# Twelve dense steps instead of eight between the levels of a GLA pair, levels in turn on VectorE, the first pair's output after the second pair's states, v copies at high priority

## The chip, the cores and the metric

The kernel runs on one core of a Trainium2 chip. The metric is the device time of one execution in microseconds; the time before is the median of three runs. Engines are called as in the profile: PE (TensorE), DVE (VectorE), ACT (ScalarE), POOL (GpSimd), SP (the queue that issues DMAs here).

## The reference

One layer of a bidirectional encoder, applied to two batches with the same weights: a prompt of 256 tokens and a sample of 512 tokens, width 1024.

```python
h = rmsnorm(x, norm1[l])
(gq, gk, gv, gg, glr, dq, dk, dvv, sz, sxbc, sdt) = jnp.split(h @ w_in[l], IN_OFFSETS, axis=-1)
...
x = x + jnp.concatenate([o_gla, o_diff, o_ssd], axis=-1) @ w_out[l]
h = rmsnorm(x, norm2[l])
x = x + jnp.square(jax.nn.relu(h @ w_mlp1[l])) @ w_mlp2[l]
```

Three mixers stand between `w_in` and `w_out`. The one that the change is about is `o_gla`: gated linear attention with four heads, forward and backward, in which each pair of tokens i, j is weighted by a decay for each of 64 channels:

```python
b = jnp.cumsum(gi, axis=1)
diff = b[:, :, None] - b[:, None, :]
decay = jnp.exp(jnp.where(mask[:, :, None, None], diff, -jnp.inf))
attn = jnp.einsum('bihd,bjhd,bijhd->bijh', qi, ki, decay)
```

`o_diff` is a differential attention with softmax, whose v comes from the columns `dvv`; `o_ssd` is a state space mixer behind a convolution over five tokens. Everything is float32.

## The kernel before

All 768 tokens of both batches lie side by side, as six tiles of 128 tokens (`NT`, `T`). A product with a weight is made of three matmuls in float32r on a high and a low part of both operands (`mm3`, L97 to L101).

**Dense steps.** `tm_steps` (L212) is a generator: for one unit of 256 weight columns it yields after each of the six token tiles, that is after 8 x 3 = 24 matmuls. Two tiles share one accumulator, of which there are three (`psa`, `N_ACC`, L52; `fm_unit`, which makes the convolution's products, takes from the same three), and after each second step a consumer takes the accumulator away. Four such units are chained in `rest` (L1125): the output gates of the two GLA pairs (consumer `gcons`: a tanh on ACT and a product on DVE, at high priority) and the v of the two differential pairs (`diff_v`, L825; consumer `vcons`: a copy on ACT into a tile, and a store of it to memory by SP). What `rest` has left is drawn by `diff_in` (L822) behind its own q and k units.

**GLA levels.** The heads are worked on in two pairs. `gla_within` (L408) makes the attention inside a chunk of 128 tokens in seven levels, s = 64, 32, 16, 8, 4, 2, 1, and once more for the diagonal. A level subtracts a reference from the two prefix sums (`d`, L452, two buffers of pool `d2`), takes exponentials on ACT (L463, L472), multiplies q and k by them on DVE (`eq` L464, `ek` L473, from pool `t3` with four buffers), and then multiplies small blocks on PE (`blocks`, L428: 96 matmuls of 32 columns for each of the two heads). `into_local` (L346) puts the result into `L` on DVE. Before the blocks of each level `other()` (L414) draws one dense step from `rest`; a list, `order`, ties step and blocks to each other in this order on PE. A pair draws eight steps, so two pairs draw sixteen of the 24: all twelve of the gates and four of the first v unit.

**Order.** Each engine works through its queue in the order that a planner gives it at build time. It takes the program's order as priority and its own model of durations; a block marked `tc.high_priority()` comes ahead of its place, `tc.issue_after(ins)` keeps the instructions traced inside behind `ins` on the engine of `ins`.

**Tiles that the change touches.** The pool `in` (`i3`, L69) has twelve tiles. While the second pair's levels run they hold v, q and k of the second pair (four) and the gates of both pairs (four); a copy of v in `vcons` takes one until its store has landed. Later each consumer of `diff_in` (L802) takes two, a raw and a squared one, and the convolution (L612, L623) takes two for each of its six tiles. The output of a pair is `gla_out` (L525): twelve products on DVE (L530), twelve transposes, four scalings on ACT, four stores. The states of a pair are `gla_states` (L348). In the program (L1126 to L1132) the first pair's output stands between the second pair's levels and the second pair's states.

After that come the differential attention of the prompt (`diff_in` and `diff_head` for two pairs of heads), the convolution, the state space mixer, the output product, the MLP of the prompt, and the same for the sample.

Of the kernel before, what the change touches and what calls it, by code (L numbers as in the profile page):

```python
# [14 lines left out]
AF = mybir.ActivationFunctionType  # L15
ALU = mybir.AluOpType
# [4 lines left out]
P = 128  # L21
D = 1024
KT = D // P
NT = 6
T = NT * P
# [18 lines left out]
def hybrid_kernel(ctx, tc, io):  # L44
    nc = tc.nc
    mm, act, dve, pool = nc.tensor.matmul, nc.scalar, nc.vector, nc.gpsimd
# [41 lines left out]
    def mx(name):  # L88
        return psm.tile([P, 512], F32, tag="mx", name=nm(name))
# [4 lines left out]
    def bc(ap, shape):  # L94
        return ap.to_broadcast(shape)
# [57 lines left out]
    def in_unit(c0, n=256):  # L153
        return load_unit(lambda r: [(0, n, w_in[:, r, c0:c0 + n])], (KT, n))
# [57 lines left out]
    def tm_steps(load, consume):  # L212


        w = load()
        for t0 in range(0, NT, 2):
            ps = acc("tm")
            for i in range(2):
                ts = slice((t0 + i) * P, (t0 + i + 1) * P)
                for k in range(KT):  # L220
                    last = mm3(ps[:, i * 256:(i + 1) * 256], tuple(z[:, ts] for z in hT[k]),
                               (w[0][:, k, :], w[1][:, k, :]), k == 0, k == KT - 1)
                if i == 1:
                    consume(ps.rearrange("p (t c) -> p t c", t=2), t0)
                yield last
# [35 lines left out]
    def v128(t):  # L261
        return t.rearrange("p (c w) -> p c w", w=P)
# [42 lines left out]
    def gla_v(hp):  # L305
        v = [i3("gv") for _ in range(2)]

        def vcons(ps, t0):
            with tc.high_priority():
                for h in range(2):  # L310
                    act.copy(v128(v[h])[:, t0:t0 + 2, :], ps[:, :, h * P:(h + 1) * P])

        tm_unit(in_unit(C_GV + 2 * hp * P), vcons)
        return v
# [29 lines left out]
    def into_local(L, ps, i):  # L344

        dve.copy_predicated(L, bc(masks[:, i, None, :], [P, NT, 32]), ps)  # L346
# [61 lines left out]
    def gla_within(pre, qk, rest):  # L408

        Xf, Xb, _ = pre  # L410
        q, k = qk
        order = []

        def other():  # L414
            with ExitStack() as behind:
                for ins in order[-1:]:
                    behind.enter_context(tc.issue_after(ins))
                order.append(next(rest))

        A = [v128(c4("A", n=T)) for _ in range(2)]
        L = t2("L", n=12 * 32).rearrange("p (h c i) -> p h c i", h=2, c=NT)
        pool.memset(L, 0.0)
        k3 = v128(k)

        def blocks(ps, h, w, left, right, across):  # L428

            hs = slice(64 * h, 64 * h + 64)  # L430
            with tc.issue_after(order[-1]):
                for c in range(NT):
                    for b in range(P // w):
                        o = b ^ across
                        last = mm(ps[w * b:w * b + w, c, :], lhsT=left[hs, c, w * b:w * b + w],
                                  rhs=right[hs, c, w * o:w * o + w], start=True, stop=True)
            order.append(last.ins)

        for li, s in enumerate(LEVELS):
            nb = T // (2 * s)  # L440
            d = d2("d")

            def parts(t):

                return t.rearrange("p (b r i) -> p b r i", r=2, i=s)

            D = [parts(d[:, i * T:(i + 1) * T]) for i in range(2)]

            for i, X in enumerate((Xb, Xf)):
                x = parts(X)  # L450
                ref = x[:, :, 1, 0:1] if i == 0 else x[:, :, 0, s - 1:s]
                dve.tensor_tensor(D[i].rearrange("p b r i -> p b (r i)"), X.rearrange("p (b i) -> p b i", i=2 * s),  # L452
                                  bc(ref, [P, nb, 2 * s]), ALU.subtract)
            eq = t3("eq")

            def halves(t):
                return t.rearrange("p (b r i) -> p r b i", r=2, i=s)

            if s <= 32:

                own = d[:, :2 * (T + s)].rearrange("p (r x) -> p r x", r=2)[:, :, :T]
                own = own.rearrange("p r (b i) -> p r b i", i=2 * s)[:, :, :, :s]
                act.activation(own, own, AF.Exp, scale=-0.0625)  # L463
                dve.tensor_tensor(halves(eq), own, halves(q), ALU.mult)  # L464
            else:
                for i in range(2):
                    act.activation(D[i][:, :, i], D[i][:, :, i], AF.Exp, scale=-0.0625)
                    dve.tensor_tensor(parts(eq)[:, :, i], D[i][:, :, i], parts(q)[:, :, i], ALU.mult)
            if s > 1:
                ek = t3("ek")  # L470
                for i in range(2):
                    act.activation(D[1 - i][:, :, i], D[1 - i][:, :, i], AF.Exp, scale=0.0625)  # L472
                    dve.tensor_tensor(parts(ek)[:, :, i], D[1 - i][:, :, i], parts(k)[:, :, i], ALU.mult)  # L473
            else:
                ek = k
            left, right = v128(ek), v128(eq)
            other()
            if s == 64:
                for h in range(2):
                    ps = mx("att")[:, :NT * 64].rearrange("p (c i) -> p c i", c=NT)  # L480
                    blocks(ps, h, 64, left, right, 1)
                    act.copy(A[h][0:64, :, 64:128], ps[0:64])
                    act.copy(A[h][64:128, :, 0:64], ps[64:128])
                continue
            for h in range(2):
                ps = mx("att")[:, :NT * 32].rearrange("p (c i) -> p c i", c=NT)
                blocks(ps, h, 32, left, right, int(s == 32))
                if s < 32:
                    into_local(L[:, h], ps, LOCAL.index(s))
                    continue  # L490
                for b in range(4):
                    o = 32 * (b ^ 1)
                    act.copy(A[h][32 * b:32 * b + 32, :, o:o + 32], ps[32 * b:32 * b + 32])

        q2 = t3("q2")
        act.activation(q2, q, AF.Copy, scale=2.0)
        other()
        for h in range(2):
            ps = mx("att")[:, :NT * 32].rearrange("p (c i) -> p c i", c=NT)
            blocks(ps, h, 32, k3, v128(q2), 0)  # L500
            into_local(L[:, h], ps, LOCAL.index(0))
            for b in range(4):
                act.copy(A[h][32 * b:32 * b + 32, :, 32 * b:32 * b + 32], L[32 * b:32 * b + 32, h])

        return A

# [18 lines left out]
    def gla_out(hp, core, sg):  # L525
        o_sb, rs = core
        for h in range(2):
            for c in range(NT):
                ov = v128(o_sb[h])[:, c, :]
                dve.scalar_tensor_tensor(ov, ov, rs[:, h, c:c + 1], v128(sg[h])[:, c, :], op0=ALU.mult, op1=ALU.mult)  # L530
            oT = t3("oT")
            for (a, b) in ((0, 4), (4, 6)):
                ps = mx("goT")
                for c in range(a, b):
                    nc.tensor.transpose(ps[:, (c - a) * P:(c - a + 1) * P], v128(o_sb[h])[:, c, :], ident)
                act.activation(oT[:, a * P:b * P], ps[:, :(b - a) * P], AF.Copy, scale=half[:, 40:41])
            for sq, (a, b) in enumerate(SEQS):
                nc.sync.dma_start(out=mixg[sq][2 * hp + h], in_=oT[:, a * P:b * P])
# [286 lines left out]
    def diff_v(p):  # L825
        def vcons(ps, t0):
            v = i3("dv", n=512).rearrange("p (t c) -> p t c", t=2)
            act.copy(v, ps)  # L828
            nc.sync.dma_start(out=dvd[p][t0 // 2], in_=v)
        return tm_steps(lambda: in_unit(C_DV + 256 * p), vcons)  # L830

# [184 lines left out]
    v = gla_v(0)  # L1016
# [67 lines left out]
    pre = [gla_gates(hp) for hp in range(2)]  # L1084
# [36 lines left out]
    states = gla_states(pre[0], qk, v)  # L1121
    qk1, v1 = gla_qk(1), gla_v(1)
    gates = [gla_gate_out(hp) for hp in range(2)]
    v_steps = [diff_v(p) for p in range(2)]
    rest = chain(gates[0][1], gates[1][1], *v_steps)  # L1125
    A = gla_within(pre[0], qk, rest)  # L1126
    core = gla_sum(A, states, v)
    A = gla_within(pre[1], qk1, rest)
    gla_out(0, core, gates[0][0])
    states = gla_states(pre[1], qk1, v1)  # L1130
    core = gla_sum(A, states, v1)
    gla_out(1, core, gates[1][0])  # L1132

# [122 lines left out]
    def feature_tiles(t):  # L1256

        return [tuple(z[:, 256 * (k % 4):256 * (k % 4) + 256] for z in B[f"{k // 4 + 1}{t + 1}"]) for k in range(KT)]

    halves = [feature_tiles(t) for t in range(2)]  # L1260
# [169 lines left out]
```

## Time and profile before

| | |
|---|---|
| time before | 1137.02 us, median of three (1133.65 to 1139.05) |
| profiled execution | 1138.52 us, its span 1136.7 us |
| granted clock of PE, mean | 0.983 |
| PE busy | 1086.8 us, 96% of the span |
| PE weight loads busy | 986.5 us, 87% |
| DVE busy | 804.3 us, 71% |
| ACT busy | 622.3 us, 55% |
| POOL busy | 126.8 us, 11% |

The page gives one execution. Busy time of PE is modelled, since matmuls overlap; what tells more is where PE is idle, what ended the idle time, and which clock was granted (1.0 is 2.4 GHz, 0.5 is 1.2 GHz). A row in which two numbers stand ahead of the engine begins with the start and the duration in us; a count follows x; an idle time ahead of an instruction stands in brackets with the instruction that ended it.

### The profile page before, as it was taken

The page shows a single profiled execution, that of the slowest core. Times are in us where ns is not written, and L with a number is a line of the kernel's source. Part 1 is how long each engine was busy: PE and PEld are TensorE (multiplying, and loading weights), DVE is VectorE, ACT ScalarE, POOL GpSimd, SP SyncE. Part 2 cuts the span into 40 slices and gives each one's busy share as a digit, 9 for nine tenths or more (in the row PEclk, how much of TensorE's full clock was granted, in tenths as well). Part 3 has the DMA queues.
Part 4 walks back from the last instruction along what each step waited for, and adds up shares of the span by engine and source line. Part 5 has one row for each costly group of instructions (what it writes and reads, how often), then busy time and mean ns, then how long its engine had stood idle before and what let it go on. Part 6 is the DMA issues. An engine that isn't in the chain of part 4 may idle for free.

```text
span 1136.7 us, 20939 instructions
## 1 busy us (share of the span) xinstructions
PE 1086.8 (96%) x8372; PEld 986.5 (87%) x8372; DVE 804.3 (71%) x1414; ACT 622.3 (55%) x1216; POOL 126.8 (11%) x184
## 2 busy tenths in 40 slices
PE   7999879999999998899999999998999999999998
PEld 7999779999889986788878897787988998998997
DVE  6579975474687577887687787756886756756752
ACT  7487574664267236756766673434544543543541
POOL 1001012220400280110101102200000000000000
PEclk9999898999999999899999999999999999999999
DMA  6212101172425355345545457642252342242212
GB/s 201 87 42 76 40 22 67 38 232 73 130 83 152 104 172 171 112 148 170 184 139 176 159 175 257 214 148 74 96 185 76 93 126 78 93 131 74 93 38 74
DMA packets 118647, 136.49 MB, mean 120 GB/s; under 512 B 8935, under 2 KB 86789, under 8 KB 118549
## 3 DMA queue, kind: packets, MB, share of 16 engines
q1 hardware_dynamic: 118517, 135.14, 37.6%
q8 instruction: 66, 1.08, 0.4%
q14 instruction: 32, 0.26, 0.1%
q10 hardware_dynamic: 32, 0.01, 0.0%
HBM read 121.44 MB, written 13.68 MB: 119 GB/s over the span
## 4 chain that ended last, share of the span: by engine, by line
PE 66%; DVE 13%; DMA 10%; ACT 7%; issue 2%; POOL 1%; SPq 0%; ACTq 0%; DVEq 0%; POOLq 0%
PE tp L99 8%; PE tp L100 8%; PE tp L101 8%; PE X L1288 7%; DMA wr<-in_w_mlp 5%; PE tm L99 4%; PE tm L101 4%; PE tm L100 4%; PE fm L99 4%; PE fm L100 3%; PE Z L1288 3%; PE fm L101 3%; DVE wl L136 3%; ACT wh L135 2%; DMA er<-scr 2%
## 5 line engine op out<-in xcount | busy, mean ns | idle before, releaser
L136 DVE TENSOR_TENSOR wl<-wr,wh 128x1024 fp32r<-128x1024 f32 x130 | 160.0, 1245 | 65.1 <-ACT wh L135 64.7
L135 ACT CAST wh<-wr 128x1024 fp32r<-128x1024 f32 x138 | 141.7, 1049 | 108.4 <-DMA wr<-in_w_mlp 58.8
L99 PE MATMUL tm<-wh,hTh 128*128 128x256 f32 x576 | 166.5, 290 | 0.9 <-ACT xp L620 0.8
L101 PE MATMUL tm<-wh,hTl 128*128 128x256 f32 x576 | 166.0, 289 | 0.0
L100 PE MATMUL tm<-wl,hTh 128*128 128x256 f32 x576 | 164.5, 286 | 0.0
L99 PEld LDWEIGHTS tm<-wh,hTh 128*128 128x128 f32 x576 | 110.6, 192 | 3.0 <-ACT xp L620 1.0
L100 PEld LDWEIGHTS tm<-wl,hTh 128*128 128x128 f32 x576 | 110.9, 193 | 0.4 <-DVE wl L136 0.2
L101 PEld LDWEIGHTS tm<-wh,hTl 128*128 128x128 f32 x576 | 110.6, 192 | 0.1
L1381 DVE TENSOR_TENSOR xres<-tp,xres 128x512 f32<-128x512 f32 x56 | 38.6, 690 | 55.1 <-PE tp L101 54.6
L99 PE MATMUL fm<-h,wh 128*128 128x256 f32 x256 | 71.7, 282 | 1.8 <-ACT relu L993 1.8
L100 PE MATMUL fm<-h,wh 128*128 128x256 f32 x256 | 71.8, 282 | 0.0
L101 PE MATMUL fm<-h,wl 128*128 128x256 f32 x256 | 71.1, 282 | 0.6 <-DVE wl L136 0.6
L99 PE MATMUL fm<-hTh,wh 128*128 128x384 f32 x160 | 55.8, 349 | 2.8 <-ACT dv L828 2.6
L100 PE MATMUL fm<-hTl,wh 128*128 128x384 f32 x160 | 55.0, 343 | 0.0
L101 PE MATMUL fm<-hTh,wl 128*128 128x384 f32 x160 | 54.7, 342 | 0.0
L947 DVE TENSOR_TENSOR xres<-tp,xres 128x512 f32<-128x512 f32 x60 | 40.3, 685 | 16.3 <-PE tp L101 16.2
L100 PE MATMUL tp<-wl,u 128*128 128x512 f32 x128 | 51.0, 398 | 0.5 <-DVE wl L136 0.5
L99 PE MATMUL tp<-wh,u 128*128 128x512 f32 x128 | 49.8, 401 | 0.9 <-ACT wh L135 0.8
L101 PE MATMUL tp<-wh,u 128*128 128x512 f32 x128 | 50.6, 395 | 0.0
L99 PEld LDWEIGHTS fm<-h,wh 128*128 128x128 f32 x256 | 48.2, 188 | 2.5 <-ACT relu L993 2.1
L101 PEld LDWEIGHTS fm<-h,wl 128*128 128x128 f32 x256 | 47.8, 188 | 1.0 <-DVE wl L136 0.8
L100 PEld LDWEIGHTS fm<-h,wh 128*128 128x128 f32 x256 | 48.2, 188 | 0.6
(429 smaller groups left out, 3089.3 us busy)
## 6 DMA issues: line engine op xcount, KB each, us to landing
wr<-in_w_mlp SPq DMA_DIRECT2D x100, 512.0 KB
wr<-in_w_in SPq DMA_DIRECT2D x30, 512.0 KB
wb<-in_w_mlp SPq DMA_DIRECT2D x28, 512.0 KB
wr<-in_w_out SPq DMA_DIRECT2D x24, 512.0 KB
ar<-scr SPq DMA_DIRECT2D x6, 512.0 KB
er<-scr SPq DMA_DIRECT2D x6, 512.0 KB
x<-in_x_sample SPq DMA_DIRECT2D x4, 512.0 KB
wr<-in_w_in SPq DMA_DIRECT2D x8, 256.0 KB
```

The lines of the kernel that those rows point to most:

```text
L99: mm(out, lhsT=lh, rhs=rh, start=first, stop=False)
L100: mm(out, lhsT=lh, rhs=rl, start=False, stop=False)
L101: return mm(out, lhsT=ll, rhs=rh, start=False, stop=last).ins
L135: act.copy(hi, raw)
L136: dve.tensor_tensor(lo, raw, rd(hi), ALU.subtract)
L947: dve.tensor_tensor(xres[t][:, cs], ps, xres[t][:, cs], ALU.add)
L1288: mm(out, lhsT=a[l][:, k, c], rhs=b[r][:, k, :], start=first and j == k == z == 0, stop=j == 1 and k == 3 and z == 2, skip_group_check=True)
L1381: dve.tensor_tensor(xres[t][:, cs], ps, xres[t][:, cs], ALU.add)
```

## The change

`other()` is called twice before the blocks of the levels s = 16, 8, 4 and 2, so a pair draws twelve steps and the two pairs draw all 24; `diff_in` finds `rest` empty. A list `ends` keeps the last DVE multiply of each level: the subtractions of a level are issued behind the last multiply of the level before last, the multiplies of q behind the last multiply of the level before. The copy of v from its accumulator gets high priority. `gla_out` of the first pair stands after `gla_states` of the second.

```diff
-        order = []
+        order, ends = [], []
+
+        def behind(n):
+
+            return tc.issue_after(ends[-n]) if len(ends) >= n else ExitStack()
...
-                dve.tensor_tensor(D[i].rearrange("p b r i -> p b (r i)"), X.rearrange("p (b i) -> p b i", i=2 * s),
-                                  bc(ref, [P, nb, 2 * s]), ALU.subtract)
+                with behind(2):
+                    dve.tensor_tensor(D[i].rearrange("p b r i -> p b (r i)"), X.rearrange("p (b i) -> p b i", i=2 * s),
+                                      bc(ref, [P, nb, 2 * s]), ALU.subtract)
...
+            with behind(1):
+                if s <= 32:
...
+                    act.activation(own, own, AF.Exp, scale=-0.0625)
+                    end = dve.tensor_tensor(halves(eq), own, halves(q), ALU.mult)
+                else:
+                    for i in range(2):
+                        act.activation(D[i][:, :, i], D[i][:, :, i], AF.Exp, scale=-0.0625)
+                        dve.tensor_tensor(parts(eq)[:, :, i], D[i][:, :, i], parts(q)[:, :, i], ALU.mult)
             if s > 1:
                 ek = t3("ek")
                 for i in range(2):
                     act.activation(D[1 - i][:, :, i], D[1 - i][:, :, i], AF.Exp, scale=0.0625)
-                    dve.tensor_tensor(parts(ek)[:, :, i], D[1 - i][:, :, i], parts(k)[:, :, i], ALU.mult)
+                    end = dve.tensor_tensor(parts(ek)[:, :, i], D[1 - i][:, :, i], parts(k)[:, :, i], ALU.mult)
             else:
                 ek = k
+            ends.append(end.ins)
             left, right = v128(ek), v128(eq)
-            other()
+            for _ in range(2 if 1 < s < 32 else 1):
+                other()
...
             v = i3("dv", n=512).rearrange("p (t c) -> p t c", t=2)
-            act.copy(v, ps)
+            with tc.high_priority():
+                act.copy(v, ps)
             nc.sync.dma_start(out=dvd[p][t0 // 2], in_=v)
...
     A = gla_within(pre[1], qk1, rest)
+    states = gla_states(pre[1], qk1, v1)
     gla_out(0, core, gates[0][0])
-    states = gla_states(pre[1], qk1, v1)
     core = gla_sum(A, states, v1)
```

## Rows read from the trace of the kernel before

**Rows 1.** Busy time of each engine in stretches of the execution. Columns: stretch and its length in us, then PE, PE weight loads, DVE, ACT and POOL busy in us (instructions), granted clock, DMA share, GB/s. The first is the GLA levels, the second reaches to the end of the first differential head pair, the third is the convolution with the second head pair.

```profile
102.90:186.60 83.70, 71.71 (x1850) 68.57 (x1850) 64.04 (x120) 48.97 (x118) 4.93 (x5) 0.92 0.13 37
186.60:296.50 109.90, 109.04 (x930) 108.52 (x931) 60.30 (x147) 60.85 (x142) 23.14 (x24) 1.00 0.33 100
296.50:366.00 69.50, 62.85 (x361) 60.70 (x360) 58.77 (x120) 43.83 (x98) 9.43 (x23) 0.95 0.44 131
```

**Rows 2.** PE's waits over the whole execution, the longest in total: who waited for whom, us in total, times, longest.

```profile
PE att L435 <- DVE ek L473: 11.0, 2, 6.4
```

**Rows 3.** PE's timeline in the GLA levels: two matmuls of one dense step, and the first small blocks (or output product) of some levels.

```profile
104.48 0.28 PE L100 MATMUL tm<-wl,hTh 128*128 128x256 f32 x1
...
107.07 0.28 PE L101 MATMUL tm<-wh,hTl 128*128 128x256 f32 x1
...
124.35 1.43 PE L435 MATMUL att<-eq,ek 64*32 64x32 f32 x96 [4.58 <-DVE ek L473]
...
130.08 1.05 PE L435 MATMUL att<-eq,ek 64*32 64x32 f32 x96
...
134.06 1.05 PE L435 MATMUL att<-eq,gk 64*32 64x32 f32 x96
...
142.97 0.49 PE L516 MATMUL gout<-gv,A 128*128 128x128 f32 x2 [0.83 <-ACT A L503]
...
171.52 1.42 PE L435 MATMUL att<-eq,ek 64*32 64x32 f32 x96 [6.45 <-DVE ek L473]
...
177.52 1.05 PE L435 MATMUL att<-eq,ek 64*32 64x32 f32 x96
...
181.53 1.05 PE L435 MATMUL att<-eq,gk 64*32 64x32 f32 x96
```

**Rows 4.** Busy times as in Rows 1, in stretches of 4 us, behind the two long waits.

```profile
124.00:128.00 4.00, 3.65 (x106) 3.62 (x107) 4.00 (x7) 1.64 (x3) 0.00 (x0) 0.50 0.02 4
...
172.00:176.00 4.00, 4.00 (x92) 3.94 (x82) 2.95 (x5) 1.64 (x2) 0.44 (x1) 0.50 0.10 30
```

**Rows 5.** DVE's timeline ahead of the two waits.

```profile
121.37 0.55 DVE L473 TENSOR_TENSOR ek<-d,gk 128x384 f32<-128x384 f32 x1
121.84 0.95 DVE L464 TENSOR_TENSOR eq<-d,gq 128x768 f32<-128x768 f32 x1
122.71 1.49 DVE L473 TENSOR_TENSOR ek<-d,gk 128x384 f32<-128x384 f32 x3
...
167.42 1.21 DVE L136 TENSOR_TENSOR wl<-wr,wh 128x1024 fp32r<-128x1024 f32 x1
...
169.03 0.94 DVE L464 TENSOR_TENSOR eq<-d,gq 128x768 f32<-128x768 f32 x1
169.90 1.48 DVE L473 TENSOR_TENSOR ek<-d,gk 128x384 f32<-128x384 f32 x3
```

**Rows 6.** DVE's instructions in the GLA levels (102.9 to 186.6 us), grouped by line: count, busy us, mean ns of one, idle before.

```profile
L340 DVE SCALAR_TENSOR_TENSOR gg<-gg,tm 128x256 f32<-128x256 f32 x12 | 5.0, 415 | 1.8 <-ACT gg L199 1.7
...
L530 DVE SCALAR_TENSOR_TENSOR o<-o,grs,gg 128x128 f32<-128x128 f32 x12 | 3.3, 333 | 0.0
```

**Rows 7.** ACT's timeline in the GLA levels: two exponentials of one level, and the first two copies of v.

```profile
139.80 0.85 ACT L463 ACTIVATE d<-d 128x768 f32<-128x768 f32 x1 [0.28 <-DVE d L452]
140.55 0.51 ACT L472 ACTIVATE d<-d 128x384 f32<-128x384 f32 x1
...
177.63 0.59 ACT L828 COPY dv<-tm 128x512 f32<-128x512 f32 x1 [2.46 <-PE tm L101]
185.62 0.59 ACT L828 COPY dv<-tm 128x512 f32<-128x512 f32 x1 [7.40 <-PE tm L101]
```

**Rows 8.** ACT's waits in the GLA levels (102.9 to 186.6 us), as in Rows 2.

```profile
ACT d L463 <- DVE d L452: 12.5, 8, 5.1
...
ACT dv L828 <- PE tm L101: 9.9, 2, 7.4
```

**Rows 9.** ACT's timeline: the first and the last of the four copies of v that come after the GLA levels.

```profile
240.77 0.56 ACT L828 COPY dv<-tm 128x512 f32<-128x512 f32 x1
...
301.71 0.59 ACT L828 COPY dv<-tm 128x512 f32<-128x512 f32 x1 [1.13 <-DMA dvd<-dv]
```

**Rows 10.** PE's timeline: the first transposes of the first differential head pair, and three matmuls of the convolution's first tile.

```profile
240.30 0.39 PE L857 MATMUL qT<-ident,dqkv 128*128 128x128 f32 x2
...
299.47 0.69 PE L99 MATMUL fm<-hTh,wh 128*128 128x384 f32 x1 [2.57 <-ACT dv L828]
...
303.01 0.33 PE L101 MATMUL fm<-hTh,wl 128*128 128x384 f32 x1
...
306.13 0.34 PE L101 MATMUL fm<-hTh,wl 128*128 128x384 f32 x1
```

**Rows 11.** Waits between 186 and 300 us, as in Rows 2: those of DVE for the first differential head pair's matmuls.

```profile
DVE dmx L883 <- PE sc L882: 7.2, 3, 3.3
...
DVE oes L908 <- PE ss L905: 5.6, 2, 3.4
...
DVE sq L915 <- PE rb L913: 3.0, 1, 3.0
```

**Rows 12.** DVE's timeline: the first instruction on the q and k of the second differential pair.

```profile
291.57 0.68 DVE L809 TENSOR_REDUCE dss<-dsq 128x8 f32<-128x512 f32 x1
```

**Rows 13.** What the instructions on the convolution's tile xp waited for, us and times.

```profile
  DMA dkd<-dqk: 7.6, 2
```

More of the change, by code (lines that the diff above doesn't have):

```diff
@@ L411, in gla_within @@
         q, k = qk
-        order = []
+        order, ends = [], []
+        def behind(n):
+            return tc.issue_after(ends[-n]) if len(ends) >= n else ExitStack()
         def other():
-            with ExitStack() as behind:
+            with ExitStack() as stack:
                 for ins in order[-1:]:
-                    behind.enter_context(tc.issue_after(ins))
+                    stack.enter_context(tc.issue_after(ins))
                 order.append(next(rest))
@@ L457, in halves @@
                 return t.rearrange("p (b r i) -> p r b i", r=2, i=s)
[L459 to L468, printed above, removed]
+            with behind(1):
+                if s <= 32:
+                    own = d[:, :2 * (T + s)].rearrange("p (r x) -> p r x", r=2)[:, :, :T]
+                    own = own.rearrange("p r (b i) -> p r b i", i=2 * s)[:, :, :, :s]
+                    act.activation(own, own, AF.Exp, scale=-0.0625)
[4 more added lines that the diff above has]
+                        dve.tensor_tensor(parts(eq)[:, :, i], D[i][:, :, i], parts(q)[:, :, i], ALU.mult)
             if s > 1:
```

## The prediction

> **What bounds the kernel now.** I read four views in this order. First the busy times by stage: between the first small attention block (102.9 us) and the last (186.6) PE works only 71.7 of 83.7 us at a mean granted clock of 0.92, while in the next 110 us it is idle for 0.9 us [rows 1]. So the kernel is bound by PE nearly everywhere, and the stretch of the GLA levels is the place where PE is lost. Second, PE's waits by cause: the largest is the small attention matmuls (L435) waiting for the second multiply of a level (ek, L473), 11.0 us in two waits [rows 2]. Third, PE's timeline places them: 4.58 us before the block at 124.35 (first pair) and 6.45 us before the one at 171.52 (second pair) [rows 3], both the fifth level, s = 4. Fourth, the clock: after each wait PE runs at the granted clock 0.50, the lower of its two levels, 1.2 GHz [rows 4].
>
> What one wait costs in all: a level (one dense step and 192 small matmuls) takes 3.98 us from 130.08 to 134.06, but 5.73 from 124.35 to 130.08, so the low clock costs 1.75; the second pair's takes 6.00 against 4.01, so 1.99 [rows 3]. The waits are worth 4.58 + 1.75 + 6.45 + 1.99 = **14.8 us**.
>
> Why VectorE is late there: in order, it did one ek of level 4, then the eq of level 2 (0.96 us), then the three remaining ek in one run that ends at 124.20; in the second pair the same, ending at 171.38 [rows 5]. PE was let go right after each run. So some 0.95 + 2 x 0.5 = 1.95 us of level 2 stood ahead of what PE waited for. In the second pair 12 instructions of the first pair's output (L530, 3.3 us, [rows 6]) and a weight's split, which ends at 168.6, stood there as well [rows 5].
>
> **The change, part by part.** (1) Twelve dense steps instead of eight. A dense step is 24 matmuls; 22 spacings from 104.48 to 107.07 [rows 3] are 0.118 us each, so 2.82 us a step. Four more steps a pair, eight in all, put 22.6 us of PE work into this stretch and take it out of the stretch behind, where before had the last two steps of the first v unit and all six of the second (their four copies run from 240.77 to 301.71, [rows 9]). PE's work is the same in sum; only what fills idle time counts. In the first pair PE would come to level 4 three steps later, at 119.77 + 8.5 = 128.2. VectorE's end moves from 124.2 by -1.95 for the order, and by +1.7 (four more gate products at 0.415, [rows 6]) and +2.4 (the next unit's split, two of 1.21, [rows 5]) that come earlier: 126.4. Margin 1.8 us, so the wait goes. In the second pair PE gains the same 8.5 us of cover for a wait of 6.45, the order gives 1.95 and the output that moves away 3.3: margin 7.3 us. What comes next there is the wait of the output product for A (0.83 us, [rows 3]), which stays.
>
> (2) Levels in turn. No instruction is added, only an order on VectorE. The two d buffers already hold a level's subtractions behind the multiplies of the level before last, so only the order of the multiplies is new. Queued behind such a multiply are gate products and splits; they wait at most for one level's exponentials. Its 1.95 us is counted in (1), and it isn't a gain of its own.
>
> (3) First pair's output behind the second pair's states. Its 12 products, 12 transposes, 4 scalings and 4 stores on SP's queue move back; its two gate tiles and two o tiles live longer. After 186.6 PE is full [rows 1], so both what moves there and the earlier start of the states are hidden by dense steps: I count nothing, with 3.3 us as the bound on either side [rows 6].
>
> (4) v copies at high priority. Six copies of 0.59 us on ScalarE and six stores on SP, four of each earlier than before. ScalarE is busy 49.0 of 83.7 us in the stretch [rows 1]; I count nothing and give the risk below.
>
> (5) What the moved steps leave behind. This is the term that no row shows, so I bound it. At 299.47 PE waits 2.57 us for a v copy [rows 10], at a place where the "in" tiles are used up: the second head pair's q and k hold six raw and six squared tiles, all twelve, until VectorE begins on them at 291.57 [rows 12], when the first head pair is nearly through. After the change no v copy wants a tile there, but the convolution's xp does; that it waits for stores of k is in the trace already [rows 13]. PE can run ahead by the three accumulators: v gave 3 x 5.64 = 16.9 us, the convolution gives 3 x 24 matmuls at 0.173 (18 spacings from 303.01 to 306.13, [rows 10]), 12.5 us. The two other v steps (5.6) are gone too. If the first head pair's chain, from 240.30 [rows 10] to 291.57, is rigid, 22.6 - 12.5 = 10.1 us of it lie bare. If it speeds up, nothing does: VectorE waits in it 7.2 + 5.6 + 3.0 = 15.8 us for PE, which dense steps ahead in its queue hold up [rows 11], more than the 10.1. So the cost is between 0 and 10.1 us. Neither end is nearer to a row, since the 15.8 us are on the chain in part only; I take half, 5.0. The 2.57 us and its low clock (11 spacings in 3.54 us instead of 1.90, so 1.64, [rows 10]) I leave as they are.
>
> **Sum.** -14.8 + 5.0 = -9.8 us. The profiled execution was 1138.5 us (span 1136.7), 1.5 above the median of the three, 1137.0; against it the sum gives 1128.7, against the median 1127.2. I forecast **1127.2**, with 1121 to 1131 as its own range.
>
> A rule that bears on (5): the trace has the one wait at 299.47, while the twelve tiles are held. The Trainium skill, "Perfetto Trace Analysis", section Optimization Strategy, says that a gap that repeats on an engine that should be saturated can mean that there isn't enough memory for the next tile to be allocated. By that rule the gap would come again for each convolution tile, which is the second rival; so far the trace shows it once.
>
> **The rivals.** *All of it is gained.* The chain of the first heads speeds up and the wait at 299.47 goes with the v copies: -14.8 - 2.57 - 1.64 = -19.0, 1118.0. For it speak the 15.8 us of waits for PE; against it, that xp wants the same tiles.
>
> *Given back at the convolution.* The chain is rigid, 10.1 us. Besides, from 296.5 to 366 VectorE is busy 58.8 us and PE 62.9 [rows 1]; with 12.5 us of PE's work drawn ahead, VectorE's 58.8 exceeds the 57.0 that are left, 1.8 us, and one more fall of the clock is 1.6. -14.8 + 10.1 + 3.4 = -1.3, 1135.7. For it speaks that VectorE is the busier engine there; against it, that the gates' dense steps behind the convolution can move up.
>
> *Slower: ScalarE held up by v copies.* ScalarE sat 2.46 us and 7.40 us in front of a v copy until its matmuls were done [rows 7]. If a copy that comes earlier stands ahead of the exponentials of the level whose blocks PE wants next, then after the steps PE waits for the copy 0.59, exponentials 0.85 + 2 x 0.5 [rows 7] and multiplies 1.95: 4.4 us and some 1.9 of low clock, 6.3 a level. One level costs less than the gain; two leave +2.8; three give +9.1, 1146.1: slower from the third on, of four doubled levels. Against it: twelve gate tanh at high priority already stand in this stretch and none shows in ScalarE's waits; of matmuls it waited for v copies alone, 9.9 us in two waits [rows 8].
>
> A rule beside this: the Trainium skill, "TensorE: Matmul & The Clock Gate", section Architectural detail, says that ScalarE and VectorE take their queues strictly in order. The trace agrees: nothing of ScalarE runs in the 7.40 us. That speaks against high priority for a copy, by this rival and its chance.
>
> *Not as it says.* The order holds, but a split and a gate product (2.8 us) fill the place of level 2's multiplies in the first pair: over the margin of 1.8, 1.0 of wait and 1.75 of low clock stay: 1127.2 + 2.8 = 1130.0.
>
> **How the numbers follow.** Chances: forecast 0.50, all gained 0.17, given back 0.20, slower 0.09, not as it says 0.04. The range reaches from 1116 (all gained, and up to 2 us of the earlier states) to 1140, past the one that gives back by the 3.3 us of (3) and the spread of the runs; some 0.15 is left out, most of it in the slower case. A measurement of this kernel tells about 0.5%, 5.7 us, from no change. Faster by more: the forecast, all gained and not as it says, less 0.04 for the forecast's upper end, 0.67. Within: given back and that end, with 0.01 of the slower case, 0.25. Slower: 0.08.
>
> **What would show it.** Step (1): no wait of L435 for L473 over 1 us, twelve dense steps between a pair's first and last level, the stretch some 7.8 us longer (22.6 - 14.8) at a clock near 1.00. (2): eq of level 2 only after both ek of level 4. (3): L530 of the first pair behind the states' multiplies. (4): ScalarE's waits for v copies with no exponentials late behind them. (5): the first convolution matmul waits 2 to 12 us for an xp copy. I am wrong if L435 still waits several us, if PE is idle for more than 12 us where the convolution begins, or if new waits stand in the sample stage, on which this change has no hold.

## The result, and the profile after

The kernel with the change took **1129.81 us** (median of 6 runs, 1128.80 to 1133.07) against 1136.39 us of the kernel before (6 runs, 1133.65 to 1139.05): a ratio of **0.9943, 95% interval 0.9926 to 0.9960**, or 6.6 us less by the medians. The forecast was 1127.2. The profiled execution took 1128.8 us (span 1127.0), 9.7 less than that of before, so the trace shows some 3 us more of a gain than the medians do.

First the stages, with the columns of [rows 1]: the GLA levels from their first small block to their last, from there to the end of the stretch in which the second row of [rows 1] ended, the convolution with the second head pair, and 12 us inside that.

```profile
102.40:191.70 89.30, 89.14 (x1945) 86.24 (x1944) 72.51 (x128) 56.11 (x126) 9.55 (x17) 1.00 0.19 58
191.70:296.50 104.80, 101.69 (x916) 100.95 (x916) 58.06 (x150) 58.46 (x142) 20.06 (x16) 1.00 0.34 107
296.50:366.00 69.50, 54.68 (x335) 53.75 (x335) 60.17 (x121) 43.86 (x98) 7.33 (x19) 0.90 0.38 118
318.00:330.00 12.00, 0.91 (x5) 0.79 (x5) 11.81 (x19) 7.04 (x16) 0.17 (x3) 0.68 0.35 99
```

The levels are full now: 0.16 us of PE is idle, and the clock is 1.00 where it was 0.92. The loss has moved: in the third stretch PE is busy 54.7 us where it was 62.9, at 0.90 where it was 0.95, and for 11 of the 12 us from 318 PE does nothing while VectorE has 0.2 us to spare.

PE's waits between 187 and 400 us, as in [rows 2]:

```profile
PE wT L899 <- DVE pr L896: 11.1, 1, 11.1
PE tm L99 <- ACT xp L628: 3.5, 1, 3.5
PE fm L99 <- ACT xp L628: 2.2, 1, 2.2
```

Its timeline: the first and the last small block, the first convolution matmul, the wait for xp, and the long wait, which stands in the second head pair, in front of the transposes of the first probabilities.

```profile
102.42 0.80 PE L439 MATMUL att<-eq,ek 64*64 64x64 f32 x21
...
191.71 1.05 PE L439 MATMUL att<-q,gk 64*32 64x32 f32 x96
...
278.29 0.34 PE L99 MATMUL fm<-hTh,wh 128*128 128x384 f32 x1
...
295.17 0.44 PE L99 MATMUL fm<-hTh,wh 128*128 128x384 f32 x1 [2.18 <-ACT xp L628]
...
317.76 0.38 PE L891 MATMUL sc<-kz,qs 128*128 128x256 f32 x1 [0.23 <-DVE kz L876]
329.24 0.66 PE L899 MATMUL wT<-ident,pr 128*128 128x128 f32 x2 [11.09 <-DVE pr L896]
```

The same two blocks of before started at 102.88 and at 185.51:

```profile
185.51 1.05 PE L435 MATMUL att<-q,gk 64*32 64x32 f32 x96
```

So the levels grew from 82.63 to 89.29 us, by 6.7, while 22.6 us of dense steps came in: **15.9 us gained**. Where the prompt's output product (tp from mo) begins, less of it is left. That product's matmuls and those of block X, in the last stage, before and then after (count, least, median and most ns, first and last start):

```profile
L99 PE MATMUL tp<-wh,mo x32: 387/394/404, 407.4 to 432.0; 128*128 128x512 f32 x32
...
L1288 PE MATMUL X<-bh,un x192: 277/280/288, 802.6 to 1104.6; 128*128 128x256 f32 x192
```

```profile
L99 PE MATMUL tp<-wh,mo x32: 387/394/404, 400.6 to 425.6; 128*128 128x512 f32 x32
...
L1297 PE MATMUL X<-bh,un x192: 277/280/287, 793.0 to 1094.9; 128*128 128x256 f32 x192
```

It is 407.4 - 400.6 = 6.8 us there. The levels began 0.46 us earlier, so 15.9 + 0.5 - 6.8 = **9.6 us were given back** between 192 and 400 us. At block X the profiled pair lies 802.6 - 793.0 = 9.6 us apart, equal to that figure by chance; the medians keep 6.6.

What VectorE does in the 12 us, from its timeline:

```profile
319.13 0.42 DVE L892 TENSOR_REDUCE dmx<-sc 128x1 f32<-128x256 f32 x1
...
320.11 1.23 DVE L136 TENSOR_TENSOR wl<-wr,wh 128x1024 fp32r<-128x1024 f32 x1
321.36 0.42 DVE L892 TENSOR_REDUCE dmx<-sc 128x1 f32<-128x256 f32 x1
321.71 1.22 DVE L136 TENSOR_TENSOR wl<-wr,wh 128x1024 fp32r<-128x1024 f32 x1
322.84 1.02 DVE L634 SCALAR_TENSOR_TENSOR zh<-xp,half,zh 128x772 f32<-128x772 f32 x1
323.77 0.95 DVE L654 SCALAR_TENSOR_TENSOR bcm<-xp,zh 128x772 f32<-128x772 f32 x1
...
325.69 1.94 DVE L634 SCALAR_TENSOR_TENSOR zh<-xp,half,zh 128x772 f32<-128x772 f32 x2
...
327.68 1.02 DVE L634 SCALAR_TENSOR_TENSOR zh<-xp,half,zh 128x772 f32<-128x772 f32 x1
328.61 0.48 DVE L896 SCALAR_TENSOR_TENSOR pr<-pr,dratio 128x256 f32<-128x256 f32 x1
```

The convolution's multiplies (zh, 1.0 us each), its bcm and two splits (wl) stand between the two maxima (dmx) and pr. PE began the convolution at 278.29, before it did at 299.47 [rows 10]: 21.2 us earlier; the first pr of the second head pair came only 2.0 us earlier (328.61 against 330.63 in before):

```profile
330.63 0.48 DVE L887 SCALAR_TENSOR_TENSOR pr<-pr,dratio 128x256 f32<-128x256 f32 x1
```

### The profile page after: what moved, and what is told of

The parts are those of the page before. It is cut to its first block, busy times and chain, and to the rows that moved or that the text cites. A ratio compares the mean times of both kernels' runs of the same rounds, so it can differ in the third digit from the quotient of the medians.

```text
span 1127.0 us, 20930 instructions
## 1 busy us (share of the span) xinstructions
PE 1080.3 (96%) x8372; PEld 982.7 (87%) x8372; DVE 806.0 (72%) x1414; ACT 622.2 (55%) x1216; POOL 126.2 (11%) x184
## 4 chain that ended last, share of the span: by engine, by line
PE 76%; DVE 8%; ACT 6%; DMA 5%; POOL 2%; issue 2%; SPq 0%; ACTq 0%; DVEq 0%; POOLq 0%
PE tp L100 9%; PE tp L99 9%; PE tp L101 9%; PE X L1297 7%; PE fm L99 5%; PE fm L100 5%; PE fm L101 5%; PE tm L99 4%; PE tm L101 4%; PE tm L100 4%; PE Z L1297 4%; DMA wr<-in_w_mlp 2%; DVE wl L136 2%; DMA er<-scr 2%; PE Y L1297 2%
## 5 line engine op out<-in xcount | busy, mean ns | idle before, releaser
L1390 DVE TENSOR_TENSOR xres<-tp,xres 128x512 f32<-128x512 f32 x56 | 38.6, 690 | 55.4 <-PE tp L101 54.7
L99 PE MATMUL fm<-h,wh 128*128 128x256 f32 x256 | 73.0, 287 | 1.9 <-ACT relu L1002 1.9
L100 PE MATMUL fm<-h,wh 128*128 128x256 f32 x256 | 73.2, 287 | 0.0
L99 PEld LDWEIGHTS fm<-h,wh 128*128 128x128 f32 x256 | 49.5, 194 | 2.6 <-ACT relu L1002 2.1
L100 PEld LDWEIGHTS fm<-h,wh 128*128 128x128 f32 x256 | 49.5, 193 | 0.6
```

Source lines behind the costliest of these rows:

```text
L99: mm(out, lhsT=lh, rhs=rh, start=first, stop=False)
L100: mm(out, lhsT=lh, rhs=rl, start=False, stop=False)
L1390: dve.tensor_tensor(xres[t][:, cs], ps, xres[t][:, cs], ALU.add)
```

## The experiments

Each was timed in five rounds against the kernel before. Behind them stands one account: the gain in the levels is real, and part of it is lost again because PE is short of dense steps where the second head pair begins. What theory A and its rival are is said anew with each. The times in us below are the ratio times before's 1138.

**One part or some parts alone.** First the twelve steps alone on the kernel before (a_steps_only), and the other three parts without them (b_no_steps).

```diff
 a_steps_only (against before)
-            other()
+            for _ in range(2 if 1 < s < 32 else 1):
+                other()
```

> The kernel before with twelve dense steps a pair and nothing else of the change (no order of the levels, the first pair's output early, plain v copies). Theory A (the dense steps are the cover; the other three parts add little): both waits of the small blocks for ek stay away, the GLA stretch ends 6 to 7 us later than before's 186.6 as in the changed kernel, time 0.994 of before, within 0.003. Rival B (the order of the levels or the later output is what takes the waits away, the steps only move work): a wait of L435 of 3 us or more is left, mostly in the second pair, where 3.3 us of the first pair's output stand ahead, and the time is 0.998 of before or more.

```diff
 b_no_steps (against after)
-            for _ in range(2 if 1 < s < 32 else 1):
-                other()
+            other()
```

> The changed kernel with eight dense steps a pair, so the other three parts alone (levels in turn, output later, v copies at high priority). Theory A (cover): at most the 1.95 us of level 2 go from each wait and 3.3 us from the second pair's, so waits of about 2.6 and 1.2 us are left, 7 us of 11 go; since the v steps stay where they were, nothing is given back: 0.993 to 0.997 of before. Rival B: no wait over 0.5 us is left in the GLA stretch and the time is 0.987 of before, since 14.8 us are gained and no filler is lost behind.

Steps alone: 0.9962 (0.9946 to 0.9979), 4.3 us, inside theory A's range. No small block waits for ek. The wait that comes instead has another name, a convolution transpose (xtmp) behind zh; the waits between 100 and 400 us:

```profile
PE xtmp L643 <- DVE zh L639: 9.4, 1, 9.4
PE fm L99 <- ACT xp L621: 4.0, 1, 4.0
```

Without the steps: **0.9936 (0.9915 to 0.9957)**, 7.3 us, as much as the whole change within the intervals, and in theory A's range. Here the levels' waits (gout is their output product) are smaller and not gone, and no wait over 1.7 us follows:

```profile
PE att L439 <- DVE ek L479: 5.2, 2, 2.8
PE gout L523 <- ACT A L510: 3.9, 1, 3.9
```

So the twelve steps, which my sum gave nearly all of the gain, aren't needed for it; on top of the other three parts they exchange one loss for another of about the same size.

**The order of the levels**, taken out of after (c_no_turn), and alone on before (h_turn_only).

```diff
 c_no_turn (against after)
-            return tc.issue_after(ends[-n]) if len(ends) >= n else ExitStack()
+            return ExitStack()
```

> The changed kernel without the order of the levels on VectorE (both subtractions and multiplies free). Theory A: with twice the dense steps the planner takes the levels in turn of itself, so this is a repeat of the changed kernel: 0.994 of before, within 0.002, and ek of level 4 ahead of eq of level 2. Rival B: the order is needed, eq of level 2 comes between the two ek of level 4 again, PE reaches level 4 too early by about 0.2 us in the first pair, and the time is 0.996 or more.

> The kernel before with the order of the levels' multiplies alone: eight dense steps, output early, plain v copies. Theory A (each wait of the small blocks falls by the 1.95 us of level 2's multiplies that stood in front): waits of some 2.7 and 4.5 us for ek stay, each with a stretch at half clock, 3 to 4 us less in the stretch of the levels, and at 1133 to 1136 the time is 3 to 4 us below before's. Rival B (the order takes no more than it moves on): within 1.5 us of before's.

Out of after: 0.9942 (0.9921 to 0.9963), and every engine has the same instructions in the same order as in after: with twelve steps the order says nothing new, and this run is a repeat of after. Alone (h_turn_only is before with the added order and nothing else): 0.9958 (0.9941 to 0.9975), 4.8 us. The waits fell from 11.0 us to

```profile
PE att L439 <- DVE ek L479: 6.1, 2, 3.3
```

The theory said 2.7 and 4.5; it is 2.8 and 3.3. It is a gain of its own where the steps aren't doubled.

**The first pair's output**, late on before alone (i_out_late_only), and early again in after (d_out_early).

```diff
 i_out_late_only (against before); d_out_early is the reverse, against after
-    gla_out(0, core, gates[0][0])
     states = gla_states(pre[1], qk1, v1)
+    gla_out(0, core, gates[0][0])
```

> The kernel before with the first pair's output product behind the second pair's states, and nothing else changed. Theory A (its 3.3 us on VectorE stood ahead of the second pair's level 4): the first pair's wait stays at 4.6 us, the second's falls from 6.45 to some 3 us, and the time is 3 to 5 us below before's. Rival B (the split of a weight and the gate products that ended at 168.6 set the second wait as much): the second wait stays over 5 us and the time is within 1.5 us of before's.

> The kernel after, with the first pair's output product ahead of the second pair's states again (the third part of the change undone). Theory A (with twelve steps the output hides in the levels, and where it stands only reshuffles what is drawn behind): within 3 us of after's, and no wait of the small blocks over 1 us. Rival B (by itself that part took 4 to 5 us, by what it changed in the convolution's stage and not in the levels): 4 to 6 us above after's, with more waiting in the convolution's stage.

Alone: 0.9953 (0.9933 to 0.9972), 5.3 us, and neither theory's way. The wait in the levels is what it was (first row, 100 to 400 us), as the rival said of it; the gain is in the convolution's stretch (second row, columns of [rows 1]), where PE works 67.1 us at clock 1.00 instead of 62.9 at 0.95. Before's wait of 2.57 us for a v copy [rows 10] is gone; why it went with this edit wasn't tried.

```profile
PE att L435 <- DVE ek L473: 11.0, 2, 6.5
```

```profile
296.50:366.00 69.50, 67.11 (x429) 65.94 (x429) 58.65 (x114) 46.80 (x104) 5.25 (x21) 1.00 0.45 139
```

Undone in after: 0.9960 (0.9945 to 0.9976), 1.9 us above after, with overlapping intervals, so that its worth inside the change is open. The convolution's wait is then that of a_steps_only, 9.1 us of xtmp for zh.

**Fewer steps.** Only the levels 8 and 4 get two dense steps, so that 20 of 24 are drawn, not 24 (f_two_levels).

```diff
-            for _ in range(2 if 1 < s < 32 else 1):
+            for _ in range(2 if 2 < s < 16 else 1):
```

> The changed kernel with double steps at two levels only, s = 8 and 4: ten steps a pair, so four steps of the last v unit (11.3 us) stay behind for the differential attention. Theory A (what was given back is lost filler there): the GLA stretch has no wait over 1 us (cover 5.6 us against 4.58 - 1.95 in the first pair and 6.45 - 1.95 - 3.3 in the second), and the 11.09 us wait of wT for pr at 329 shrinks by most of 11.3 us, so 0.986 to 0.990 of before. Rival C (what was given back is VectorE's order, convolution ahead of the second head pair's ratio): the wait stays at 8 us or more and the time is 0.992 to 0.996.

0.9968 (0.9953 to 0.9983), 3.6 us. The long wait shrank as theory A has it, from 11.1 to 3.0 us; but others came up, and the time, 2.8 us above after's with overlapping intervals, is by the ratio above the ranges of both theories. Part of the loss moved ahead of the convolution, into a stretch in which after has PE busy for 101.69 us at clock 1.00 (second row, columns of [rows 1]).

```profile
PE xtmp L650 <- DVE zh L646: 3.8, 2, 2.3
PE wT L899 <- DVE pr L896: 3.0, 1, 3.0
```

```profile
191.70:296.50 104.80, 98.54 (x782) 95.94 (x781) 51.87 (x142) 51.84 (x127) 19.85 (x13) 0.95 0.30 93
```

**Is the long wait a matter of order on VectorE?** (j_zh_behind)

```diff
                 for k in range(1, 5):
-                    dve.scalar_tensor_tensor(zh, xp[:, k:k + 772], ...
+                    with tc.issue_after(prs[4]) if j != 4 else ExitStack():
+                        dve.scalar_tensor_tensor(zh, xp[:, k:k + 772], ...
```

Here prs[4] is the first pr of the second head pair, and j = 4 the convolution's first tile.

> The kernel after, with one order more: the convolution's multiplies (zh, four a tile) of the second to sixth tile may go on VectorE only behind the first pr of the second head pair. Theory A (the 11.1 us wait of wT for pr is a matter of order on VectorE: about twelve zh multiplies of 1.0 us and one bcm stand in front of the ratio and pr): the wait falls under 2 us, no other takes its place, and the time is 5 to 9 us below after's. Rival B (VectorE has more work there than PE has left, 291 to 334 us without a pause in it): the wait moves to the convolution's own users, xtmp waiting for zh or the convolution's matmuls waiting for xp, 6 to 11 us together, and the time is within 2 us of after's.

0.9970 (0.9953 to 0.9986), 3.1 us above after with overlapping intervals. The first pr came 7.7 us earlier, and PE then waited for the second one as well:

```profile
321.52 0.66 PE L902 MATMUL wT<-ident,pr 128*128 128x128 f32 x2 [4.45 <-DVE pr L899]
...
330.57 0.66 PE L902 MATMUL wT<-ident,pr 128*128 128x128 f32 x2 [7.54 <-DVE pr L899]
```

11.1 us became 12.0 in two waits. With this order PE stands still elsewhere and no shorter: the rival is right that the wait only moves, though it named other places for it and a time within 2 us of after's. No other order was tried.

**Is it the missing dense steps?** Two kinds of filler: work for nothing (k_refill makes and stores the second v unit twice) and work that is due later (l_gate_first, m_gate_mid).

```diff
 k_refill (in diff_in)
         for _ in v_steps[p]:
             pass
+        if p == 1:
+            for _ in diff_v(1):
+                pass
 l_gate_first
+    ssd_gate(0)
     tail = ssd_conv((2, 0, 1), xt, bcm)
-    ssd_gate(0)
     tail()
 m_gate_mid (in ssd_conv, and the call behind it taken out)
                 if len(tails) > 1:
                     tail()
+            if u == us[0]:
+                ssd_gate(0)
```

> The kernel after, with one unit of work too much: the second v unit (six dense steps, 144 matmuls, some 16.9 us of PE) is made and stored a second time behind the second pair's q and k, so PE has dense steps to spare where the second head pair begins. Theory A (11.1 + 2.2 us of PE's waits there come only from the filler drawn ahead): the waits go under 3 us together and the time is 4 to 8 us above after's, not 17. Rival B (VectorE or ScalarE bound there, more work makes it no shorter): the 11 us wait stays or moves and the time is 14 to 19 us above after's.

> The kernel after, with the first SSD gate's unit (six dense steps, 16.9 us of PE, work that the kernel needs anyway) in the program ahead of the convolution instead of behind it. Theory A (after loses 11.1 + 2.2 us in waits between 295 and 330 because dense steps are short there, and a second v unit made for nothing there cost no time): the waits go under 3 us together and the time is 6 to 14 us below after's, if behind the convolution nothing wants the filler. Rival B (the steps are then short behind the convolution, where the first chunk's states and transposes wait for VectorE): the waits come again between 340 and 380 us, 8 us or more, and the time is within 3 us of after's.

> The kernel after, with the first SSD gate's unit behind the convolution's first pair of tiles instead of behind all three pairs. Theory A, as for the run before: the 11.1 us wait goes under 3 us, and the time is 6 to 12 us below after's. Rival B: waits of the same size behind the convolution, within 3 us of after's.

k_refill: 0.9924 (0.9900 to 0.9949). **16.9 us of useless PE work cost nothing**; the time is 2.2 us below after's with overlapping intervals, where theory A had said 4 to 8 us above. The convolution's stretch (columns of [rows 1]) and PE's longest wait from 187 to 400 us:

```profile
296.50:366.00 69.50, 67.12 (x430) 65.95 (x430) 59.59 (x114) 46.69 (x103) 5.07 (x21) 1.00 0.46 141
```

```profile
PE xtmp L650 <- DVE zh L646: 1.0, 1, 1.0
```

PE is busy 12.4 us more there than in after, in the same time, at clock 1.00. Useful filler of the same length, six steps, then gains a part of it: l_gate_first **0.9882 (0.9864 to 0.9900)**, 13.4 us below before; m_gate_mid **0.9890 (0.9870 to 0.9911)**, 12.5. They are 6.9 and 6.0 us below after's, inside theory A's ranges, the second at the edge. Both intervals lie below after's, so both beat both kernels; between them nothing is decided. PE's longest waits from 187 to 400 us in l_gate_first, then in m_gate_mid:

```profile
PE xtmp L650 <- DVE zh L646: 4.4, 2, 2.9
PE rb L922 <- DVE dg L920: 3.5, 1, 3.5
```

```profile
PE rb L924 <- DVE dg L922: 3.2, 1, 3.2
PE fm L99 <- ACT xp L628: 3.1, 2, 2.2
```

The wait for pr is under 1.5 us in both. Behind it the rival's waits do come, 9.5 us in l_gate_first (four between 339 and 372 us) and 6.4 in m_gate_mid (three), where after has one of 3.5; they cost a part, and the time that the rival drew from them is wrong.

**Does the earlier gate also help eight steps?** (p_mid_eight is m_gate_mid with the edit of b_no_steps.)

> The gate's unit behind the convolution's first pair of tiles, as in m_gate_mid, but with eight dense steps between a pair's levels; the other three parts of the change stay. Theory A (twelve steps gain some 16 us against before in the levels' stretch and cost it again where the second head pair lacks steps; with eight there is no such lack to fill): the small blocks' waits of some 5 us with their low clock are back, the earlier gate gains under 3 us, and the time is 3 to 8 us above m_gate_mid's 0.989, at 0.992 to 0.996. Rival B (the earlier gate is a gain of its own, whatever the number of steps): 5 to 7 us below the eight-step kernel's 0.9936, at 0.987 to 0.990.

1.0117 (1.0097 to 1.0137), 13.3 us slower than before: neither theory. A wait that is in none of the others came up at 399 us, the first SSD chunk's product behind an addition on GpSimd (waits of 187 to 400 us):

```profile
PE y L748 <- POOL ar L743: 16.4, 1, 16.4
PE rb L923 <- DVE dg L921: 6.6, 1, 6.6
```

So it doesn't say what the earlier gate is worth with eight steps, nor whether its gain depends on the twelve; the new wait hides that. Why the planner set the chunk's product ahead of the dense steps there wasn't tried.

## Why the prediction was right, and where it wasn't

The time lies inside the forecast's own range of 1121 to 1131, 2.6 us above the forecast. Two of the terms of the sum were off, in opposite directions: by the trace -15.9 + 9.6 = -6.3 us where the sum had -14.8 + 5.0 = -9.8. That the profiled pair lies 9.7 us apart, nearly the sum, is luck, since some 3 us of it came in the last stages.

**What bounds it: right.** PE, and the levels' stretch as the place where it is lost. The runs add that filling that place moves the loss to the next place where VectorE is behind.

**(1) Twelve steps remove the waits: right.** 15.9 us against 14.8. No L439 waits for ek, the clock is 1.00, and the stretch grew by 6.7 us, forecast 7.8. Of the 1.1 us more, the output product's wait for A is 0.6: it fell from 0.83 to 0.2 us, where I had it stay. The margins, from VectorE's timeline (the four multiplies of level 4 and level 2 in the first pair, then level 4's of the second):

```profile
120.95 1.03 DVE L479 TENSOR_TENSOR ek<-d,gk 128x384 f32<-128x384 f32 x2 [0.26 <-ACT d L478]
...
125.76 0.95 DVE L470 TENSOR_TENSOR eq<-d,gq 128x768 f32<-128x768 f32 x1
126.62 1.02 DVE L479 TENSOR_TENSOR ek<-d,gk 128x384 f32<-128x384 f32 x2
...
168.48 1.03 DVE L479 TENSOR_TENSOR ek<-d,gk 128x384 f32<-128x384 f32 x2 [0.59 <-ACT d L478]
```

The blocks that use the first and the last of these start at 127.35 and 176.86 us, so the margins are 5.4 us (forecast 1.8) and 7.3 (forecast 7.3). In the first pair the weight's split that I had put ahead of level 4 came behind it. The second one agrees by luck, see (3).

**(2) No gain of its own: right in the change, wrong alone.** Level 2's eq is behind level 4's ek, as said. With twelve steps the order changes no instruction's place; by itself it is worth 4.8 us.

**(3) Output later, nothing: the reason was wrong.** I moved 3.3 us of VectorE work out of the second pair's levels. It didn't move: the products still run in those levels, from 161.5 to 166.5 us (before from 158.8 to 162.4), ahead of level 4's multiplies, and only the transposes came later (the first at 204.5 us, before at 186.5). Most of the products, before and then after:

```profile
158.81 2.96 DVE L530 SCALAR_TENSOR_TENSOR o<-o,grs,gg 128x128 f32<-128x128 f32 x11
...
163.52 2.97 DVE L538 SCALAR_TENSOR_TENSOR o<-o,grs,gg 128x128 f32<-128x128 f32 x11
```

A later place in the program is not a later place on the engine, where the planner may still take the work early. Alone this part gained 5.3 us, more than my bound of 3.3 (the interval, 3.2 to 7.6, just reaches it), and in the convolution's stretch, which I hadn't looked at for it.

**(4) v copies: nothing, as far as seen.** ScalarE waits 7.2 us in two for v's matmuls (9.9 in [rows 8]), and no block waits behind it; the slower rival didn't come. The priority by itself wasn't timed.

**(5) Lost filler, 5.0 of 0 to 10.1: this is the term that failed.** It measured 9.6 us, near the end that I called rigid, but that it stayed inside the bound is luck, since most of it was lost at a place that the bound doesn't cover. The first head pair's chain was nearly rigid: from its first transposes to VectorE's first work on the second pair's q and k it took 48.6 us, before 51.3 ([rows 10], [rows 12]).

```profile
239.98 0.38 PE L866 MATMUL qT<-ident,dqkv 128*128 128x128 f32 x2
...
288.56 0.68 DVE L817 TENSOR_REDUCE dss<-dsq 128x8 f32<-128x512 f32 x1
```

PE ran ahead by 72 matmuls of the convolution, the three accumulators, and only then waited 2.2 us for xp; that is where the sum put the wait, though my sign named the first matmul. But 11.1 us came one stage later, in the second head pair. My bound on how far PE can run ahead stopped at the convolution's first accumulators, and I weighed only the first head pair's chain. My sign of being wrong, over 12 us of idle PE where the convolution begins, was drawn too narrowly as well: PE is idle for 14.8 us between 296.5 and 366, most of it 40 us behind the convolution's first matmul. PE was 21.2 us ahead at the convolution's start, used up what stood there by 318 us, and met a VectorE with no time to spare.

The second rival, given back at the convolution, had more of the mechanism, the busy VectorE with its 58.8 us, and put 13.5 us on it. The Trainium skill's rule of the repeating gap ("Perfetto Trace Analysis", section Optimization Strategy) isn't borne out here: there are two waits for xp, 2.2 and 3.5 us, not one for each convolution tile, and the long one isn't for memory.

That PE has room for dense steps there is shown by k_refill, and that useful ones gain time there, by l_gate_first and m_gate_mid; that VectorE's order isn't the cause, by j_zh_behind for the one order tried. The number of steps left there isn't all of it: f_two_levels left four and gained nothing over after. That a chain over VectorE sets the end of that stage is only argued, from its 11.81 busy us in 12.

The last stages gave 3 us in the profiled pair that the medians don't show. About 1 us of it is PE's busy time where the matmuls of fm from bh begin (granted clock 0.82 from 784 to 803 us in before, 0.91 from 776 to 794 in after); why the clock differs is open, and so is the rest.

## What to carry to other kernels

Filler that is drawn forward to cover one wait can be missing at a later one: before moving it, look at the next stage in which PE's queue meets a busy VectorE, and ask which dense work, due later still, can go there. To see whether a gap is only missing filler, put useless work into it: if the time stays, useful work moved there can be a gain (here six steps, 16.9 us, brought 6 to 7 us on top of the change). Parts of a change don't add up: three of the four alone gave 4.3, 4.8 and 5.3 us, all together 6.5.

## What the runs showed of the hardware that I hadn't expected

GpSimd's addition of two 128x1024 tiles had no fixed price. In the trace of m_gate_mid two of them took 4.29 and 2.37 us, in that of p_mid_eight the pair took 11.11, the longer one 8.07; VectorE's timeline shows it at work on the same kind of tiles (ar, er) during the long ones, in p_mid_eight on the convolution's zh as well, and in m_gate_mid idle from 384.6 to 387.8 us, around the one of 2.37. That this is what slows it was not tried.

```profile
379.36 4.29 POOL L744 TENSOR_TENSOR ar<-ar,er 128x1024 f32<-128x1024 f32 x1 [4.76 <-DVE ar L743]
384.66 2.37 POOL L744 TENSOR_TENSOR ar<-ar,er 128x1024 f32<-128x1024 f32 x1 [1.01 <-DVE ar L743]
```

```profile
391.03 11.11 POOL L743 TENSOR_TENSOR ar<-ar,er 128x1024 f32<-128x1024 f32 x2 [5.96 <-DVE ar L742]
```
